# Hybrid attention step on one core: queries and keys transposed in fp32 and split from PSUM, context heads of a chunk in one operation

## The chip, the cores and the metric

The kernel runs on one core of a Trainium2 chip. TensorE (PE; its weight loads have a row of their own, PEld), VectorE (DVE), ScalarE (ACT) and GpSimd (POOL) work in parallel; SyncE (SP) issues the DMAs. The metric is the device time of one execution in microseconds (us), the median of several runs; below 0.5% a difference can't be told from none.

## The reference

One inference step with four layers over 128 context tokens and 512 latent tokens, width 1024, 16 query heads and 4 key/value heads of 64. Per layer:

```python
u = rms_norm(h, norm_pre) * (1 + scl) + shift          # scl, shift, gate from SiLU(cond) @ w_mod
q, k, v, z = split(u @ w_in)                            # 1024, 256, 256, 1024 columns
q, k = rms_norm per head (times q_norm / k_norm), rotary positions on latent tokens (layers 0, 1, 3)
o = softmax(q k^T / 8) v        # context tokens read context keys only;
                                # latent tokens read latent keys (all, a band, or a neighbourhood) and 128 cached context keys
h = h + gate * rms_norm((o * silu(z)) @ w_out, norm_post)
```

The keys and values of the context tokens are outputs too. All of it is fp32.

## The kernel before

**Precision.** TensorE takes a 32-bit type that it multiplies in one pass with rounded operands (F32R in the code, "fp32r"). The kernel splits each fp32 operand into a rounded part `hi` and a rest `lo` and adds the products of the parts, so each projection runs three fp32r matmuls for one. Weights are split as they arrive (`start_w`, helper `split`, lines 261 and 262), activations in `start_part` and `split_og`.

**Staging.** A layer runs `kv_chunk` (projection of keys and values for five token tiles of 128), then two chunks `c` of eight query heads and two key heads each: `q_chunk` (five token tiles), `z_block` (gate), four `lat_pair` (two heads each: scores, softmax, transposes of the probabilities, attention times values), and `ctx_heads` (the context tokens' own attention, two groups `gg` of four heads). After both chunks come `split_og` and `out_phase` (output projection, residual, and the next layer's input).

**Queries.** For each token tile `q_chunk` takes the normed queries `qn` [128 tokens, 8 heads, 64] in two halves of four heads. Per half ACT writes `hi` into `hl[:, :, 0:64]` (line 613), DVE or POOL writes `lo` into `hl[:, :, 64:128]` (line 615), PE transposes the four 128x128 blocks in fp32r into a PSUM tile (line 620), and one ACT or DVE copy of 512 columns brings it to `q` (line 256, helper `evac`). So `q[:, head]` has the 64 `hi` rows on partitions 0 to 63 and the 64 `lo` rows on 64 to 127.

**Keys.** `k_stack` makes one key tile for two key heads: `hi` and `lo`, each written twice side by side (lines 544 and 545, 256 columns each), four fp32r transposes (line 553), one copy of 512 columns to `kst[:, g, i, columns]` (`i` is 0 for `hi`, 1 for `lo`; both halves of the partitions hold the same 64 rows). A score is then two fp32r matmuls that accumulate, one with `hi` keys and one with `lo` keys. In chunk 0 `k_stack` is called from `kv_chunk`; the other two key heads are kept in `kn2` (line 591), and in chunk 1 six calls build a new `kst` from it (line 1001). There is one `kst` buffer.

**Context heads.** Per group `gg`: scores, softmax, four fp32 transposes (line 826), a copy, four fp32 matmuls of attention times values into a PSUM tile (line 834; two instructions each), and one DVE operation of 256 columns that multiplies the result into the gate (line 839).

**Order of the work.** Each operation is recorded by `S.op` with planned durations and the engines that may run it. `Sched.emit` then writes the program by a greedy list scheduling: each operation's due time is its running index plus an offset of its part (`ORDER`, as 'ks' -170, 'qt' -410), and it goes out when engines, buffers and dependencies allow by the planned times (`LAT`, `TURN`, `DISLIKE`). In `TURN` the kinds of PE work are M (fp32r matmul), R (fp32r transpose), T (fp32 transpose), C (attention times values), E (modulation). PSUM has four buffers "B", shared by projections, transposes and attention times values, and two "S". The order of every engine is therefore the planner's, and it is made anew when an operation is added or removed. All DMAs go through SP's queue in order of their issue.

## Time and profile before

Three runs: 1394.93, 1398.39 and 1403.29 us, median 1398.39. The profiled execution took 1400.58 us, of which 1398.5 us is the span from the first to the last instruction; 2.1 us lie around it.

| | busy us | share | instructions |
|---|---|---|---|
| PE matmul | 1357.7 | 97% | 9464 |
| PE weight load | 1122.3 | 80% | 9464 |
| DVE | 954.7 | 68% | 2300 |
| ACT | 758.6 | 54% | 1854 |
| POOL | 266.8 | 19% | 306 |

A matmul's record is longer than its turn on the engine, since consecutive ones overlap: the time that one costs is read from one start to the next in a timeline, not from its mean duration. The mean granted TensorE clock is 0.998 of 2.4 GHz.

### The profile page before, as it was taken

How to read it: one execution, taken by the hardware profiler on the slowest of the kernel's cores; microseconds unless marked ns; L12 is line 12 of the kernel's file. 1: busy time of each engine (PE TensorE's matmuls, PEld its weight loads, DVE VectorE, ACT ScalarE, POOL GpSimd, SP SyncE). 2: the span in 40 equal slices, each digit the busy share in tenths (PEclk: the TensorE clock that was granted, in tenths of full speed). 3: DMA queues.
4: the chain of work that ended last, by engine and by line, in shares of the span. 5: the costliest groups of instructions: out<-in, count | busy, mean ns of one | idle time of the engine just before them, and what ended most of it. 6: DMA issues, size and time to landing. Idle time of an engine off the chain costs nothing.

```text
span 1398.5 us, 25496 instructions
## 1 busy us (share of the span) xinstructions
PE 1357.7 (97%) x9464; PEld 1122.3 (80%) x9464; DVE 954.7 (68%) x2300; ACT 758.6 (54%) x1854; POOL 266.8 (19%) x306
## 2 busy tenths in 40 slices
PE   6999999999999999999999999999999999999998
PEld 3788887888778887887878888888778888778876
DVE  4777667765587786777486676578488876577653
ACT  4556565554355565666354567468345555465641
POOL 1122012010032102201033541441033210021100
PEclk9999999999999999999999999999999999999999
DMA  8522222224532402324542522342633210111032
GB/s 305 175 69 84 61 91 84 69 87 140 181 115 67 147 30 91 125 92 161 161 125 73 157 57 91 98 141 85 196 126 101 91 53 10 61 52 41 31 123 103
DMA packets 73323, 145.11 MB, mean 104 GB/s; under 512 B 8752, under 2 KB 13936, under 8 KB 73200
## 3 DMA queue, kind: packets, MB, share of 16 engines
q1 hardware_dynamic: 73200, 143.50, 31.6%
q8 instruction: 74, 1.21, 0.4%
q14 instruction: 49, 0.40, 0.1%
HBM read 131.90 MB, written 11.57 MB: 103 GB/s over the span
## 4 chain that ended last, share of the span: by engine, by line
PE 83%; DVE 6%; ACT 4%; DMA 3%; issue 3%; POOL 0%; SPq 0%; DVEq 0%; POOLq 0%; ACTq 0%
PE B L497 21%; PE B L634 14%; PE B L780 8%; PE B L773 8%; PE S L901 8%; PE B L901 6%; PE S L698 5%; PE S L724 4%; PE B L383 3%; PE B L620 2%; PE S L497 1%; DVE w L262 1%; DMA raw<-in_w_mod 1%; DMA raw<-in_w_in 1%; PE B L451 1%
## 5 line engine op out<-in xcount | busy, mean ns | idle before, releaser
L307 POOL TENSOR_TENSOR sm<-sm,mhalf 128x1 f32<-128x1 f32 (+2 forms) x100 | 122.1, 1223 | 573.2 <-DVE sm L302 291.5
L497 PE MATMUL B<-w,uB 128*128 128x512 f32 x816 | 207.4, 401 | 0.0
L256 ACT ACTIVATE pt<-B 128x512 f32<-128x512 f32 (+1 forms) x228 | 126.9, 570 | 121.0 <-PE B L773 110.8
L497 PEld LDWEIGHTS B<-w,uB 128*128 128x128 f32 x816 | 149.2, 188 | 31.8 <-DVE uB L262 0.4
L634 PE MATMUL B<-uB,w 128*128 128x384 f32 x768 | 166.0, 348 | 0.6 <-DVE gate L642 0.3
L773 PE MATMUL B<-ident,p 128*128 128x128 f32 x1088 | 159.4, 276 | 3.1 <-ACT pt L256 2.3
L261 ACT ACTIVATE w<-raw 128x512 fp32r<-128x512 f32 x224 | 135.0, 627 | 30.2 <-PE B L901 8.0
L773 PEld LDWEIGHTS B<-ident,p 128*128 128x128 f32 x1088 | 125.1, 141 | 23.7 <-issue 13.6
L262 DVE TENSOR_TENSOR w<-raw,w 128x512 fp32r<-128x512 f32 x193 | 130.5, 700 | 13.0 <-ACT w L261 12.4
L497 PE MATMUL B<-w,uA 128*128 128x512 f32 x528 | 135.1, 403 | 1.1 <-DVE pt L256 0.8
L703 ACT ACTIVATE p<-S,sm 128x640 f32<-128x640 f32 x128 | 101.3, 794 | 59.6 <-DVE sm L701 54.6
L780 PE MATMUL B<-pt,vt 128*64 128x256 f32 (+1 forms) x1152 | 133.0, 376 | 0.0
L634 PEld LDWEIGHTS B<-uB,w 128*128 128x128 f32 x768 | 129.6, 188 | 3.7 <-issue 1.5
L701 DVE TENSOR_REDUCE sm<-S 128x1 f32<-128x640 f32 x128 | 102.7, 819 | 37.7 <-PE S L698 36.8
L634 PE MATMUL B<-uA,w 128*128 128x256 f32 x768 | 117.6, 290 | 0.3 <-DVE modc L394 0.3
L497 PEld LDWEIGHTS B<-w,uA 128*128 128x128 f32 x528 | 96.4, 188 | 24.7 <-DVE w L262 2.1
L780 PEld LDWEIGHTS B<-pt,vt 128*64 128x64 f32 x1152 | 77.5, 137 | 46.0 <-issue 11.4
L634 PEld LDWEIGHTS B<-uA,w 128*128 128x128 f32 x768 | 102.5, 189 | 3.4 <-issue 1.8
L658 DVE TENSOR_SCALAR p<-p,sm 128x640 f32<-128x640 f32 (+2 forms) x197 | 96.9, 506 | 6.6 <-DVE sm L657 0.5
L698 PE MATMUL S<-kst,q 128*128 128x320 f32 x512 | 96.8, 320 | 2.9 <-ACT p L703 2.8
L658 POOL TENSOR_SCALAR p<-p,sm 128x640 f32<-128x640 f32 (+2 forms) x59 | 44.0, 751 | 284.3 <-DVE sm L657 236.4
L737 ACT ACTIVATE p<-p,sm 128x512 f32<-128x512 f32 (+1 forms) x128 | 83.9, 657 | 6.4 <-DVE sm L735 6.3
(148 smaller groups left out, 2216.1 us busy)
## 6 DMA issues: line engine op xcount, KB each, us to landing
raw<-in_w_in SPq DMA_DIRECT2D x160, 256.0 KB
raw<-in_w_mod SPq DMA_DIRECT2D x160, 256.0 KB
raw<-in_w_out SPq DMA_DIRECT2D x64, 256.0 KB
w<-in_w_first SPq DMA_DIRECT2D x16, 512.0 KB
xs<-q SPq DMA_DIRECT2D x15, 512.0 KB
q<-xs SPq DMA_DIRECT2D x15, 512.0 KB
q<-in_x SPq DMA_DIRECT2D x10, 512.0 KB
kst<-gs SPq DMA_DIRECT2D x8, 512.0 KB
```

The costliest lines, as they stand in the source:

```text
L256: alts = {"A": Ap(n, lambda e: e.activation(out(), in_(), AF.Copy)), "V": V(n, lambda e: e.tensor_copy(out(), in_()))}
L261: S.op([As(n, lambda e: e.activation(h(), src(), AF.Copy))], r, w)
L262: f = lambda e: e.tensor_sub(l(), src(), h().bitcast(F32))
L307: S.op([("G", 395 + 157 * n, lambda e: e.tensor_tensor(r.ap, v.ap, mhalf.ap.to_broadcast([128, n]), op=OP.pow), "pow")], r=[v, mhalf], w=[r])
L497: e.matmul(ps(), t.ap[:, s, k, off:off + 128], W[k].ap[:, w], start=k == 0 and i == 0, stop=k == 7 and i == 2)
L634: e.matmul(ps.ap[:, 0:w], W[k].ap[:, wi, 128 * f:128 * f + 128], t.ap[:, s, k, :], start=k == 0 and i == 0, stop=k == 7 and i == 2)
L658: f = lambda e, i=i, p=p, w=w: e.tensor_scalar(p.ap[:, 0:w], p.ap[:, 0:w], rs.ap[:, i:i + 1], 1.0, op0=OP.mult, op1=OP.mult)
L698: e.matmul(ps.ap[:, b, 0:320], Q[t + 1].ap[:, hh], kst.ap[:, g, s, 320 * b:320 * b + 320], start=s == 0, stop=s == 1)
L701: S.op([V(640, lambda e, ps=ps, i=i: e.tensor_reduce(negm.ap[:, i:i + 1], ps.ap[:, :, 0:320], axis=AX.XY, op=OP.max, negate=True))], r=[ps ...
L773: e.transpose(pt.ap[:, c:c + 128], p.ap[:, b:b + 128], ident.ap)
L780: e.matmul(po.ap[64 * x:64 * x + 64, 256 * half + q0:256 * half + q0 + w], vt.ap[:, kt, 64 * g:64 * g + 64], sbt.ap[:, c0:c0 + w], start=f ...
L901: e.matmul(ps(), t.ap[:, s, k, off:off + 128], W[k].ap[:, w], start=k == 0 and i == 0, stop=k == 7 and i == 2)
```

## The change

In `q_chunk` the fp32 queries themselves are transposed: four 128x128 blocks of two heads each, in fp32, into one PSUM tile. The parts are then made out of PSUM: for the even heads (x = 0, rows 0 to 63) ACT writes `hi` to `q` on the same rows and DVE writes `lo` to rows 64 to 127; for the odd heads (x = 1) `hi` is on rows 64 to 127 and `lo` on 0 to 63. Each of these four operations has 64 partitions and 512 columns. The scores wait for `(Q, hh % 2)` where they waited for `(Q, hh // 4)`.

In `k_stack` the source holds each key head twice side by side in fp32; two fp32 transposes fill half a PSUM tile, ACT writes `hi` (256 columns) and DVE `lo` (256 columns) to `kst`. The doubled source is made by an ACT copy of 256 columns into `kn2` (128 before), and for chunk 0 by a copy of 256 columns on ACT or DVE into a tile `kd`; cached keys are loaded twice, by four DMAs per layer in place of two. POOL has no part in the splits of queries and keys any more.

In `ctx_heads` the transposed probabilities of both groups are kept, the eight matmuls run as one operation into one PSUM tile, and one DVE operation of 512 columns multiplies the gate. `ORDER`, `TURN` and the other constants are as they were.

```diff
--- before.py
+++ after.py
@@ -538,32 +538,28 @@
     @S.named("ks")
     def k_stack(src, srckey, kst, ct, cap=None):
 
-        hl = tmp([128, 2, 2, 2, 64], F32R)
         tc_ = [cap, kst] if cap else [kst]
-        s = lambda: src()[:, :, None, :].to_broadcast([128, 2, 2, 64])
-        S.op([As(256, lambda e: e.activation(hl.ap[:, 0], s(), AF.Copy))], r=[srckey], w=[(hl, 0)], touch=tc_)
-        f = lambda e: e.tensor_sub(hl.ap[:, 1], s(), hl.ap[:, 0].bitcast(F32))
-        S.op([G(256, f), VL(256, f)], r=[srckey, (hl, 0)], w=[(hl, 1)], touch=tc_)
-        ps = S.buf("B", [128, 512], F32R)
+        ps = S.buf("B", [128, 512])
 
         def tr(e):
-            for i in range(2):
-                for g in range(2):
-                    c = 128 * (2 * i + g)
-                    e.transpose(ps.ap[:, c:c + 128], hl.ap[:, i, g].rearrange("p a d -> p (a d)"), identr.ap)
-        S.op([P(336, tr, "R")], r=[hl, identr], w=[ps], touch=tc_)
-        evac(512, lambda: kst.ap[:, :, :, 128 * COL[ct]:128 * COL[ct] + 128],
-             lambda: ps.ap.bitcast(F32).rearrange("p (i g c) -> p g i c", i=2, g=2), [ps], [(kst, ct)])
+            for g in range(2):
+                e.transpose(ps.ap[:, 128 * g:128 * g + 128], src()[:, g].rearrange("p a d -> p (a d)"), ident.ap)
+        S.op([P(218, tr, "T")], r=[srckey, ident], w=[ps], touch=tc_)
+        v = lambda: ps.ap[:, 0:256].rearrange("p (g c) -> p g c", g=2)
+        d = lambda i: kst.ap[:, :, i, 128 * COL[ct]:128 * COL[ct] + 128]
+        S.op([As(256, lambda e: e.activation(d(0), v(), AF.Copy))], r=[ps], w=[(kst, ct)])
+        S.op([V(256, lambda e: e.tensor_sub(d(1), v(), d(0).bitcast(F32)))], r=[ps, (kst, ct)], w=[(kst, ct)])
 
     def new_kst():
         return S.buf("kst", [128, 2, 2, 768], F32R)
 
     @S.named("kv")
     def kv_chunk(l, tabs, W):
-        kst, vt, kn2 = new_kst(), S.buf("vt", [128, 6, 256]), S.buf("kn2", [128, 6, 2, 64])
-        ck = tmp([128, 2, 64])
-        S.op([D(64, lambda e: e.dma_start(ck.ap, a["cache_k"][0, l, :, 0:2]))], w=[ck], touch=[kst])
-        S.op([D(64, lambda e: e.dma_start(kn2.ap[:, 4], a["cache_k"][0, l, :, 2:4]))], w=[(kn2, 4)])
+        kst, vt, kn2 = new_kst(), S.buf("vt", [128, 6, 256]), S.buf("kn2", [128, 6, 2, 2, 64])
+        ck = tmp([128, 2, 2, 64])
+        for x in range(2):
+            S.op([D(64, lambda e, x=x: e.dma_start(ck.ap[:, :, x], a["cache_k"][0, l, :, 0:2]))], w=[(ck, x)], touch=[kst])
+            S.op([D(64, lambda e, x=x: e.dma_start(kn2.ap[:, 4, :, x], a["cache_k"][0, l, :, 2:4]))], w=[(kn2, 4)])
         S.op([D(128, lambda e: e.dma_start(vt.ap[:, KC, :], a["cache_v"][0, l].rearrange("t h d -> t (h d)")))], w=[(vt, KC)])
         k_stack(lambda: ck.ap, ck, kst, 4)
         for tau in range(5):
@@ -588,9 +584,13 @@
             if tau == 0:
                 S.op([D(128, lambda e, kn=kn: e.dma_start(o["nk"][0, l], kn.ap))], r=[kn])
                 S.op([D(128, lambda e: e.dma_start(o["nv"][0, l].rearrange("t h d -> t (h d)"), vt.ap[:, VC, :]))], r=[(vt, VC)])
-            S.op([As(128, lambda e, kn=kn, ct=ct: e.activation(kn2.ap[:, ct], kn.ap[:, 2:4], AF.Copy))], r=[kn], w=[(kn2, ct)],
+            two = lambda k0, kn=kn: kn.ap[:, k0:k0 + 2, None, :].to_broadcast([128, 2, 2, 64])
+            S.op([As(256, lambda e, two=two, ct=ct: e.activation(kn2.ap[:, ct], two(2), AF.Copy))], r=[kn], w=[(kn2, ct)],
                  touch=[cap])
-            k_stack(lambda kn=kn: kn.ap[:, 0:2], kn, kst, ct, cap)
+            kd = tmp([128, 2, 2, 64])
+            S.op([As(256, lambda e, two=two, kd=kd: e.activation(kd.ap, two(0), AF.Copy)),
+                  V2(256, lambda e, two=two, kd=kd: e.tensor_copy(kd.ap, two(0)))], r=[kn], w=[kd], touch=[cap, kst])
+            k_stack(lambda kd=kd: kd.ap, kd, kst, ct, cap)
         return kst, vt, kn2
 
     @S.named("qt")
@@ -607,20 +607,20 @@
                 qn = rope(xr, 8, tabs, "q", tau - 1, cap)
             else:
                 qn = gscale(xr, 8, tabs, 0, cap)
-            for i in range(2):
-                hl, pt = tmp([128, 4, 128], F32R), S.buf("B", [128, 512], F32R)
-                s = lambda i=i, qn=qn: qn.ap[:, 4 * i:4 * i + 4]
-                S.op([As(256, lambda e, s=s, hl=hl: e.activation(hl.ap[:, :, 0:64], s(), AF.Copy))], r=[qn], w=[(hl, 0)],
-                     touch=[cap])
-                f = lambda e, s=s, hl=hl: e.tensor_sub(hl.ap[:, :, 64:128], s(), hl.ap[:, :, 0:64].bitcast(F32))
-                S.op([G(256, f), VL(256, f)], r=[qn, (hl, 0)], w=[(hl, 1)], touch=[cap])
-
-                def tr(e, hl=hl, pt=pt):
-                    for h in range(4):
-                        e.transpose(pt.ap[:, 128 * h:128 * h + 128], hl.ap[:, h], identr.ap)
-                S.op([P(336, tr, "R")], r=[hl, identr], w=[pt], touch=[cap])
-                evac(512, lambda i=i, q=q: q.ap[:, 4 * i:4 * i + 4].rearrange("p h t -> p (h t)"),
-                     lambda pt=pt: pt.ap.bitcast(F32), [pt], [(q, i)])
+            pt = S.buf("B", [128, 512])
+
+            def tr(e, pt=pt, qn=qn):
+                for pr in range(4):
+                    e.transpose(pt.ap[:, 128 * pr:128 * pr + 128], qn.ap[:, 2 * pr:2 * pr + 2].rearrange("p h d -> p (h d)"),
+                                ident.ap)
+            S.op([P(436, tr, "T")], r=[qn, ident], w=[pt], touch=[cap])
+            for x in range(2):
+                hi, lo = (slice(0, 64), slice(64, 128))[::1 - 2 * x]
+                d = lambda rows, x=x, q=q: q.ap.rearrange("p (r x) t -> p x r t", x=2)[rows, x]
+                v = lambda hi=hi, pt=pt: pt.ap[hi].rearrange("p (r t) -> p r t", r=4)
+                S.op([As(512, lambda e, d=d, v=v, hi=hi: e.activation(d(hi), v(), AF.Copy))], r=[pt], w=[(q, x)], touch=[cap])
+                S.op([V(512, lambda e, d=d, v=v, hi=hi, lo=lo: e.tensor_sub(d(lo), v(), d(hi).bitcast(F32)))], r=[pt, (q, x)],
+                     w=[(q, x)], touch=[cap])
             Q.append(q)
         return Q
 
@@ -697,7 +697,7 @@
                         for b in range(2):
                             e.matmul(ps.ap[:, b, 0:320], Q[t + 1].ap[:, hh], kst.ap[:, g, s, 320 * b:320 * b + 320],
                                      start=s == 0, stop=s == 1)
-                S.op([P(588, mm)], r=[(Q[t + 1], hh // 4)] + [(kst, x) for x in range(5)], w=[ps], seq="s")
+                S.op([P(588, mm)], r=[(Q[t + 1], hh % 2)] + [(kst, x) for x in range(5)], w=[ps], seq="s")
                 S.op([V(640, lambda e, ps=ps, i=i: e.tensor_reduce(negm.ap[:, i:i + 1], ps.ap[:, :, 0:320], axis=AX.XY, op=OP.max,
                                                                   negate=True))], r=[ps], w=[(negm, i)])
                 S.op([("A", 775, lambda e, ps=ps, p=p, i=i: e.activation(
@@ -722,7 +722,7 @@
                     for o, n, v in parts:
                         for s in range(2):
                             e.matmul(ps.ap[:, i, o:o + n], Q[t + 1].ap[:, hh], v(s), start=s == 0, stop=s == 1)
-                S.op([P(w * 0.88 + 14, mm)], r=[(Q[t + 1], hh // 4)] + [(kst, x) for x in BAND[t]], w=[(ps, i)], seq="s")
+                S.op([P(w * 0.88 + 14, mm)], r=[(Q[t + 1], hh % 2)] + [(kst, x) for x in BAND[t]], w=[(ps, i)], seq="s")
                 bb, bap = bias[t]
                 S.op([V(w, lambda e, i=i, w=w, p=p, bap=bap: e.tensor_tensor_reduce(
                     out=p.ap[:, 0:w], in0=ps.ap[:, i, 0:w], in1=bap(), op0=OP.add, op1=OP.max, scale=1.0, scalar=-3.0e38,
@@ -789,6 +789,7 @@
 
     @S.named("cx")
     def ctx_heads(l, c, Q, kst, vt, gate):
+        tiles = []
         for gg in range(2):
             g = 2 * c + gg
             ps = S.buf("S", [128, 2, 512])
@@ -798,7 +799,7 @@
                 for h in range(4):
                     for s in range(2):
                         e.matmul(psv()[:, h], Q[0].ap[:, 4 * gg + h], kst.ap[:, gg, s, 640:768], start=s == 0, stop=s == 1)
-            S.op([P(880, mm)], r=[(Q[0], gg), (kst, 5)], w=[ps], seq="s")
+            S.op([P(880, mm)], r=[Q[0], (kst, 5)], w=[ps], seq="s")
             negm, ssum, p = sm(4), sm(4), S.buf("p", [128, 4, 128])
             S.op([V(512, lambda e, psv=psv, negm=negm: e.tensor_reduce(negm.ap, psv(), axis=AX.X, op=OP.max, negate=True))],
                  r=[ps], w=[negm])
@@ -826,19 +827,22 @@
                     e.transpose(pt.ap[:, 128 * h:128 * h + 128], p.ap[:, h], ident.ap)
             S.op([P(432, tr, "T")], r=[p, ident], w=[pt])
             evac(512, lambda sbt=sbt: sbt.ap, lambda pt=pt: pt.ap, [pt], [sbt])
-            po, ocap = S.buf("B", [128, 512]), S.buf("cap_o")
-
-            def mv(e, po=po, sbt=sbt, g=g):
+            tiles.append(sbt)
+        po, ocap = S.buf("B", [128, 512]), S.buf("cap_o")
+
+        def mv(e):
+            for gg, sbt in enumerate(tiles):
+                g = 2 * c + gg
                 for h in range(4):
-                    x, b = h % 2, h // 2
+                    x, b = h % 2, 2 * gg + h // 2
                     e.matmul(po.ap[64 * x:64 * x + 64, 128 * b:128 * b + 128], vt.ap[:, VC, 64 * g:64 * g + 64],
                              sbt.ap[:, 128 * h:128 * h + 128], start=True, stop=True, skip_group_check=True)
-            S.op([P(505, mv, "C")], r=[sbt, (vt, VC)], w=[po], touch=[ocap])
-            gt = lambda g=g: gate.ap[:, 2 * g:2 * g + 2, 0:128]
-            keys = [(gate, (2 * g, 0)), (gate, (2 * g + 1, 0))]
-            S.op([V(256, lambda e, po=po, gt=gt: e.scalar_tensor_tensor(
-                gt(), po.ap[:, 0:256].rearrange("p (b q) -> p b q", b=2), 0.5, gt(), op0=OP.mult, op1=OP.mult))],
-                r=[po] + keys, w=keys, touch=[ocap])
+        S.op([P(1010, mv, "C")], r=tiles + [(vt, VC)], w=[po], touch=[ocap])
+        gt = lambda: gate.ap[:, 4 * c:4 * c + 4, 0:128]
+        keys = [(gate, (4 * c + b, 0)) for b in range(4)]
+        S.op([V(512, lambda e: e.scalar_tensor_tensor(
+            gt(), po.ap.rearrange("p (b q) -> p b q", b=4), 0.5, gt(), op0=OP.mult, op1=OP.mult))],
+            r=[po] + keys, w=keys, touch=[ocap])
 
     @S.named("tab")
     def tables(l):
```

## Rows read from the trace of the kernel before

**Rows 1.** The profile page: engine totals, and the 40 slices of the span (tenths) for PE and for the granted clock.

```profile
PE 1357.7 (97%) x9464; PEld 1122.3 (80%) x9464; DVE 954.7 (68%) x2300; ACT 758.6 (54%) x1854; POOL 266.8 (19%) x306
...
PE   6999999999999999999999999999999999999998
...
PEclk9999999999999999999999999999999999999999
```

**Rows 2.** The chain of work that ended last, by engine.

```profile
PE 83%; DVE 6%; ACT 4%; DMA 3%; issue 3%; POOL 0%; SPq 0%; DVEq 0%; POOLq 0%; ACTq 0%
```

**Rows 3.** Busy time in stretches: length, PE, PEld, DVE, ACT, POOL (instructions), granted clock, DMA share, GB/s. The first and last stretch of the span, two stretches of chunk 0's query projections, and the change from chunk 0 to chunk 1 in the last layer.

```profile
0.00:40.00 40.00, 28.41 (x178) 17.09 (x178) 21.08 (x67) 16.32 (x43) 4.93 (x12) 1.00 0.86 310
...
1335.00:1398.00 63.00, 56.81 (x252) 44.75 (x250) 26.50 (x47) 15.62 (x38) 2.77 (x5) 0.98 0.32 113
...
430.00:456.00 26.00, 26.00 (x131) 21.30 (x130) 16.94 (x34) 11.10 (x23) 6.65 (x4) 1.00 0.10 30
...
1084.00:1103.00 19.00, 19.00 (x97) 15.77 (x96) 14.49 (x29) 9.42 (x20) 4.95 (x3) 1.00 0.12 36
1185.00:1205.00 20.00, 17.33 (x123) 14.31 (x121) 9.40 (x20) 14.46 (x41) 0.00 (x0) 0.91 0.09 28
```

**Rows 4.** The chain from 1335 us to the end, in order of time: start, us, what. L901 is the output projection (fp32r, 512 columns), L834 a group of context heads.

```profile
1338.95 0.59 PE B L834 x8
1339.54 0.89 PE S L901 x3
1340.43 0.59 PE B L834 x8
1341.02 22.68 PE S L901 x96
1363.70 22.51 PE B L901 x96
```

**Rows 5.** Timeline of PE in layer 0's first query projections (L497, fp32r, 512 columns): start, us, what. L620 are the fp32r transposes of queries.

```profile
85.46 0.46 PE L620 MATMUL B<-identr,tmp 128*128 128x128 f32 x4
85.76 0.94 PE L497 MATMUL B<-w,uB 128*128 128x512 f32 x3
86.53 0.45 PE L620 MATMUL B<-identr,tmp 128*128 128x128 f32 x4
86.83 4.43 PE L497 MATMUL B<-w,uB 128*128 128x512 f32 x18
91.10 0.46 PE L620 MATMUL B<-identr,tmp 128*128 128x128 f32 x4
```

**Rows 6.** Timeline of PE in the second layer boundary. L451 are fp32 transposes (of the next layer's input), four at a time.

```profile
706.40 2.34 PE L901 MATMUL B<-w,uB 128*128 128x512 f32 x9
708.58 0.60 PE L451 MATMUL B<-ident,p 128*128 128x128 f32 x4
708.93 0.95 PE L901 MATMUL B<-w,uB 128*128 128x512 f32 x3
709.72 1.57 PE L497 MATMUL B<-w,uA 128*128 128x512 f32 x6
```

**Rows 7.** Timeline of PE at the start, where fp32 transposes (L451) come two at a time.

```profile
45.17 0.38 PE L451 MATMUL B<-ident,q 128*128 128x128 f32 x2
45.30 0.95 PE L497 MATMUL B<-w,uB 128*128 128x512 f32 x3
46.09 0.38 PE L451 MATMUL B<-ident,q 128*128 128x128 f32 x2
```

**Rows 8.** Groups of instructions by line and form over the whole span: out<-in, shape, count, busy us, mean ns, then the idle time of the engine before them.

```profile
L613 ACT ACTIVATE tmp<-tmp 128x256 fp32r<-128x256 f32 x80 | 29.5, 410 | 68.1 <-DVE tmp L534 41.9 <-DVE tmp L528 26.0
...
L615 DVE TENSOR_TENSOR tmp<-tmp 128x256 fp32r<-128x256 f32 x78 | 32.2, 435 | 12.9 <-ACT tmp L613 12.7
...
L256 ACT ACTIVATE q<-B 128x512 fp32r<-128x512 f32 x78 | 45.0, 595 | 31.9 <-PE B L620 31.6
...
L544 ACT ACTIVATE tmp<-tmp 128x256 fp32r<-128x256 f32 x24 | 10.0, 415 | 15.9 <-DVE tmp L528 5.8 <-DVE tmp L534 4.4 <-DMA tmp<-in_cache_k 4.2
L544 ACT ACTIVATE tmp<-kn 128x256 fp32r<-128x256 f32 x24 | 7.8, 425 | 0.0
L545 DVE TENSOR_TENSOR tmp<-kn,tmp 128x256 fp32r<-128x256 f32 x22 | 9.7, 504 | 0.0
L545 DVE TENSOR_TENSOR tmp<-tmp 128x256 fp32r<-128x256 f32 x23 | 9.6, 420 | 4.2 <-ACT tmp L544 4.0
L256 ACT ACTIVATE kst<-B 128x512 fp32r<-128x512 f32 x44 | 25.4, 597 | 14.1 <-PE B L553 13.4
L256 DVE CAST kst<-B 128x512 fp32r<-128x512 f32 x4 | 2.7, 686 | 0.9 <-PE B L553 0.9
L591 ACT ACTIVATE kn<-tmp 128x128 f32<-128x128 f32 x20 | 6.0, 298 | 0.0
...
L945 DVE TENSOR_TENSOR tmp<-B,kst 128x512 f32<-128x512 f32 x20 | 13.7, 687 | 21.0 <-ACT tmp L943 21.0
L839 DVE SCALAR_TENSOR_TENSOR gate<-B,gate 128x256 f32<-128x256 f32 x16 | 6.7, 420 | 13.4 <-PE B L834 13.4
L256 ACT ACTIVATE pm<-B 128x256 f32<-128x256 f32 x5 | 1.9, 381 | 7.6 <-PE B L346 7.5
L256 ACT ACTIVATE pm<-B 128x128 f32<-128x128 f32 x11 | 3.0, 277 | 16.8 <-PE B L383 16.8
L412 ACT ACTIVATE gsb<-B 16x128 f32<-16x128 f32 x4 | 1.0, 251 | 0.0
```

**Rows 9.** The line of the cached keys' first DMA: its issue on SP, ns (min/median/max), and who waited for it.

```profile
L565 SPq DMA_DIRECT2D tmp<-in_cache_k x4: 328/424/426, 37.5 to 1049.6; - x4
...
  ACT tmp L544: 4.2, 3
```

## The prediction

> **What bounds the kernel now.** I read the page first: the engine totals and the slices [rows 1]. The reader is to see that PE is busy for 97% of the span and in nine tenths or more of every slice but the first and the last, at a clock that is full in all of them, while DVE and ACT have 68% and 54%. Then the chain of waits [rows 2]: 83% of the way to the end is PE work, and what DVE and ACT add (10%) is scattered. Then the stretches [rows 3]: of PE's 1398.5 - 1357.7 = 40.8 us of idle time, 11.6 lie in the first 40 us and 6.2 in the last 63, which leaves 23 us for everything between. So a PE turn that goes away in the middle shortens the span by about its length, if the planner finds other work to put there; and a longer DVE or ACT operation costs nothing until it makes PE wait. Last I read what a turn costs, from one start to the next in the timelines, because the mean duration of a matmul holds its way through the array as well.
>
> **The change part by part.** The yardstick is the fp32r matmul of 512 columns: 96 in 22.51 us, 0.2345 us each [rows 4].
>
> An fp32r block of four transposes: from its start to the next matmul 0.30 us, twice, and the three matmuls behind the first take 0.77 us where three are worth 0.70, the 18 behind the second 4.27 for 4.22 [rows 5]. With that loss of about 0.06 a block costs 0.36 us.
>
> An fp32 block of four: 0.35 us to the next start, and the three matmuls behind it take 0.79 for 0.70 [rows 6]. I take 0.35 + 0.09 = 0.44. A block of two: 0.13 us, and again 0.79 for the next three [rows 7], so 0.22.
>
> Queries: 4 layers x 2 chunks x 5 tiles = 40 times, two fp32r blocks (0.72) become one fp32 block of four (0.44): 40 x 0.28 = 11.2 us off PE. Keys: per layer one tile from the cache, five from the projection and six in chunk 1, 48 in all; a block of 0.36 becomes one of 0.22: 48 x 0.14 = 6.7 us. If the trailing losses were not PE's own but chance, the blocks would be 0.60 against 0.35 and 0.30 against 0.13, which is 10.0 + 8.2, about the same.
>
> Context heads: two blocks of 0.59 us, with 0.89 for the three matmuls between them (0.19 too much) and 22.68 for 22.51 behind the second (0.17) [rows 4]. In one operation the 0.59 stays twice and one of the two losses goes: 0.19 x 8 chunks = 1.5 us. The bounds are nothing, if a chunk's two groups would have run next to each other or now wait for the second group's softmax, and 8 x 0.36 = 2.9 us.
>
> PE in sum: 11.2 + 6.7 + 1.5 = 19.4 us.
>
> DVE and ACT [rows 8]. Queries: DVE loses its subtractions (32.2 us) and two copies, some 1.4, and gets 80 subtractions of 512 columns from PSUM. No row has one on 64 partitions. The nearest of the same form is L945, 687 ns; by half the rows it could be half of that, but an ACT copy of 128 columns took 251 ns on 16 partitions and 277 on 128, so the columns set it, and I take 687: 80 x 0.687 = 55.0, which is 21.4 us more. (At half: 27.5, 6 us less than before.) ACT loses 29.5 + 45.0 and gets 80 x 0.595 = 47.6: 26.9 less. Keys: DVE loses 9.7 + 9.6 + 2.7 and gets 48 of 0.420 (as L839, one operand in PSUM) = 20.2, so 1.8 less; ACT loses 10.0 + 7.8 + 25.4 and gets 48 of 0.381 = 18.3, 24.9 less; the wider copy into kn2 adds 20 x 0.415 - 6.0 = 2.3 on ACT, and the 20 copies into kd at most 20 x 0.42 = 8.4 on either. The gates: 8 x 0.687 - 6.7 = 1.2 less on DVE. Together DVE gains 18 to 27 us, to about 975 us or 71%, and ACT loses 41 to 50, to about 713. PE's remaining work covers both. In a stretch of query projections DVE is the tighter one: 14.49 of 19 us [rows 3], with room for some 0.5 us more per tile; what that costs if the cover is gone is the third rival.
>
> What is late next: the PSUM tile of the queries. Now two tiles per token tile are each held for the transposes and one copy, 0.46 [rows 5] + 0.595 us, 2.1 in sum. Afterwards one is held for 0.60 [rows 6] + 0.595 + 0.595 + 0.687 = 2.5 us, because the two ACT copies run one after the other and the last subtraction follows. Tile-time rises by a fifth, without a new peak. Behind the waiting subtraction on DVE stand the next tile's norm and rotation, and PE waits for these only through the next tile's transposes. An odd or even head's scores now need half of that one tile, all four transposes, so a chunk's first scores come later than with the first of two blocks; the gate projections are there to fill PE.
>
> The DMAs: four for two, per layer. Their issue is 0.33 to 0.43 us on SP [rows 9], 8 more are about 3 us of a queue that waits for buffers most of the time. ACT waited 4.2 us in all for the cached keys; that can be nothing, or rise by the second issue, 0.4 us x 4 = 1.6 us, most of it where PE has other work. I take zero.
>
> Against the profiled execution: 1400.6 (span 1398.5 and 2.1 around it) - 19.4 = 1381.2. The profiled run stands 2.2 us above the median, so the median becomes **1379 us**.
>
> One rule speaks against it. Fp32 transposes stand at 0.13 us for two and 0.35 for four [rows 6, 7], 0.065 and 0.09 us each. The Trainium skill, "FP8 and Floating Point Precision" (TensorE Precision Notes), says that true fp32 takes four passes through the array; by that an fp32 transpose of 128 columns costs as much as 512 columns in one pass, and the sum turns round (the fourth rival). The trace does not agree for transposes, and the skill's "TensorE: Matmul & The Clock Gate" (Terms) has the reason: a transpose mode that is four times faster for fp32.
>
> **The rivals.**
> 1. *More than the sum.* Between the chunks of the last layer PE is idle for 2.7 of 20 us and the clock falls to 0.91 on average [rows 3]: there the six key tiles are split, transposed and copied, ACT doing 6 x 0.42 + 6 x 0.60 = 6.1 us. Afterwards ACT has 6 x 0.38 = 2.3 and DVE 2.5, and the transposes need no split before them. If that wait goes (2.7 + 0.09 x 20 = 4.5 us) and half as much in the three other layers in sum, the time is 1372. Against it: the same ACT is not full there, 14.46 of 20.
> 2. *The new order is worse.* The offsets of the parts count operations, and a query tile now records fewer of them, so everything behind shifts against its due time. For it: nothing in the profile protects the 23 us of idle time in the middle from growing. If it grows by half, 11.5 us, the time is 1391.
> 3. *DVE becomes the bound of the query stretches, slower than before.* The subtractions out of PSUM come last on the way to the scores and hold the tile. If PE waits for one of them per token tile, that is 40 x 0.687 = 27.5 us, and 1407. It decides from 19.4 / 40 = 0.49 us of waiting per tile. For it: 76% DVE in 19 us, which becomes 85% with two tiles more at 0.54 us. Against it: the other stretch has 65% [rows 3], and four PSUM tiles let PE go ahead.
> 4. *Fp32 transposes of queries and keys are dearer than those in the trace*, as dear as 512 columns of an fp32r matmul, 0.2345 us each [rows 4]: a query block 4 x 0.2345 + 0.09 = 1.03 (0.31 more than now, x 40 = 12.4), a key block 0.56 (0.20 more, x 48 = 9.6), less 1.5: 1419. Against it: every fp32 transpose in the trace [rows 6, 7].
>
> **How the numbers follow.** Forecast 0.58, its own range 1372 to 1388; more than the sum 0.07; the worse order 0.20; DVE 0.12; dearer transposes 0.03. 0.5% (7 us) is what a measurement of this kernel can tell from none, so faster means under 1391.4: the forecast, the first rival and half of the second, 0.75. Slower, over 1405.4: dearer transposes and over half of DVE, 0.10. Between them 0.15. The range reaches from 1367, below the first rival, to 1397, above the second, and leaves out most of the third and the fourth.
>
> **What would show it.** Right: PE's matmul busy time falls by 19 us or more with the idle time in the middle at 23 us or so; fp32 transposes of queries at 0.35 us to the next start; ACT near 713, DVE near 975 us; subtractions on 64 partitions at 0.69 us. Wrong: PE waiting for the subtractions out of PSUM in the query stretches; a fallen clock in more than one place; or transposes of 0.23 us each.

## The result, and the profile after

The changed kernel takes 1413.52 us (median of 4 runs, 1412.67 to 1414.15) against 1398.37: ratio 1.0101 (95% interval 1.0081 to 1.0120). By the ratio it is slower by 14 us where the prediction had 19 us less. The profiled execution took 1412.67 us, its span 1410.9.

The page of the kernel after: engine totals, the shares of the chain by engine, and the granted clock by slice.

```profile
PE 1353.6 (96%) x9208; PEld 1107.4 (78%) x9208; DVE 983.5 (70%) x2304; ACT 720.6 (51%) x1753; POOL 252.8 (18%) x287
...
PEclk9999999999999999999999998999999999999999
...
PE 77%; DVE 10%; ACT 4%; DMA 4%; issue 3%; POOL 1%; SPq 0%; DVEq 0%; POOLq 0%; ACTq 0%
```

Against [rows 1] PE has 256 matmuls fewer, but its busy time fell by 4.1 us only and its idle time rose from 40.8 to 1410.9 - 1353.6 = 57.3. DVE's part of the chain went from 6% to 10% [rows 2], and PE's fell to 77%.

Groups of the kernel after by line and form, in the columns of [rows 8]: the subtractions and copies of queries (L622, L621), and those of keys (L551, L550).

```profile
L622 DVE TENSOR_TENSOR q<-B,q 64x512 fp32r<-64x512 f32 x80 | 55.1, 689 | 25.6 <-ACT q L621 24.0
L621 ACT ACTIVATE q<-B 64x512 fp32r<-64x512 f32 x80 | 47.3, 592 | 43.2 <-PE B L614 42.5
...
L551 DVE TENSOR_TENSOR kst<-B,kst 128x256 fp32r<-128x256 f32 x48 | 19.4, 419 | 10.0 <-ACT kst L550 9.7
L550 ACT ACTIVATE kst<-B 128x256 fp32r<-128x256 f32 x48 | 17.8, 382 | 14.8 <-PE B L546 14.6
```

The durations of the single operations came as forecast. What PE waited for in the kernel after (us in all, times, longest):

```profile
PE B L346 <- DMA w<-in_w_first: 9.3, 2, 7.2
PE B L546 <- DVE kst L551: 5.1, 8, 1.6
PE B L614 <- DVE tmp L528: 4.4, 8, 0.8
PE B L634 <- DVE q L622: 3.8, 3, 1.3
...
PE S L698 <- DVE q L622: 0.8, 2, 0.4
...
PE B L773 <- DVE kst L551: 0.8, 2, 0.5
PE S L724 <- DVE q L622: 0.7, 2, 0.5
```

Three of the first four are DVE: the key transposes wait for a PSUM tile that the subtraction L551 still holds, the query transposes for the rotation before them (L528, on DVE too), and the gate projection (L634) for a tile that L622 holds. The waits for the two new subtractions, L551 and L622, make 11.2 us in all. In the kernel before, the waits of PE for the copies in their place (L256 to `kst` and `q`) made 1.0 us:

```profile
PE B L773 <- ACT kst L256: 0.4, 1, 0.4
...
PE B L553 <- ACT kst L256: 0.4, 1, 0.4
...
PE B L634 <- ACT kst L256: 0.2, 1, 0.2
```

One such wait, on the timeline of the kernel after (in order of start; start, us, what, and in brackets the idle time before it):

```profile
1254.93 0.63 PE L614 MATMUL B<-ident,tmp 128*128 128x128 f32 x4 [0.22 <-ACT pt L256]
...
1255.60 1.20 ACT L621 ACTIVATE q<-B 64x512 fp32r<-64x512 f32 x2
...
1255.97 0.68 DVE L262 TENSOR_TENSOR w<-raw,w 128x512 fp32r<-128x512 f32 x1
...
1256.83 1.39 DVE L622 TENSOR_TENSOR q<-B,q 64x512 fp32r<-64x512 f32 x2 [0.18 <-ACT q L621]
...
1258.25 0.82 DVE L701 TENSOR_REDUCE sm<-S 128x1 f32<-128x640 f32 x1
...
1258.37 1.54 PE L634 MATMUL B<-uB,w 128*128 128x384 f32 x4 [1.28 <-DVE q L622]
```

The transposes of this tile began at 1254.93 and DVE ended with it at 1258.22: held for 3.3 us, not 2.5. The two copies (L621) and the two subtractions (L622) ran one after the other: DVE was done with its weight split (L262) at 1256.65 and stood idle for 0.18 us until the second copy had ended. The 2.5 of the prediction had the first subtraction beside the second copy. Over the 40 tiles, the first subtraction began only behind the second copy in 36, mostly with DVE idle before it (the 24.0 us of idle time in the row of L622), and the hold is 3.3 us in the median. In 35 tiles the record of the first copy updates no semaphore (the signal that another engine waits for), so that nothing tells DVE of its end: the tile is held by the length of this chain, and not by a queue in front of DVE.

The change from chunk 0 to chunk 1 of layer 2 on PE (L546 are key transposes), and a window of it beside the window of the kernel before that has its own change of chunk, with key transposes (L553) from 854 to 861 us (columns as in [rows 3]; the first is after, the second before):

```profile
867.85 0.38 PE L546 MATMUL B<-ident,kn 128*128 128x128 f32 x2
869.81 0.44 PE L546 MATMUL B<-ident,kn 128*128 128x128 f32 x2 [1.58 <-DVE kst L551]
871.18 0.44 PE L546 MATMUL B<-ident,kn 128*128 128x128 f32 x2 [0.93 <-DVE kst L551]
```

```profile
870.00:880.00 10.00, 6.95 (x30) 4.42 (x31) 4.40 (x8) 4.02 (x8) 1.56 (x1) 0.64 0.00 0
```

```profile
855.00:865.00 10.00, 9.49 (x68) 7.18 (x66) 4.24 (x10) 7.62 (x21) 1.96 (x2) 1.00 0.00 0
```

PE waits for one key tile after the other, and behind these waits its granted clock falls: 0.64 on average, part of the window at 1.2 GHz. In full stretches of 20 us the profile after has six with a clock under 1.00, which cost 10.4 us in sum; before there was one (1.8 us). So of the 31.8 us between the forecast (19.4 less) and the profile (12.4 more), 16.5 are PE's idle time and up to 8.6 the clock (some of it falls on idle time); the rest is at least 6.7. The turns of the three changed groups did fall by 17.0 us, summed over the timelines from start to next start without idle time (queries 27.1 to 16.0, keys 17.1 to 12.4, context heads 9.4 to 8.2). Those of other groups rose: the gate projections (L634) by 6.9, the projections (L497) by 2.9, scores (L724) by 2.1, in part at the lower clock. Why the rest of them rose stays open.

### The profile page after: what moved, and what is told of

The parts are those of the page before. It is cut to its first block, busy times and chain, and to the rows that moved or that the text cites. A ratio compares the mean times of both kernels' runs of the same rounds, so it can differ in the third digit from the quotient of the medians.

```text
span 1410.9 us, 24794 instructions
## 1 busy us (share of the span) xinstructions
PE 1353.6 (96%) x9208; PEld 1107.4 (78%) x9208; DVE 983.5 (70%) x2304; ACT 720.6 (51%) x1753; POOL 252.8 (18%) x287
## 3 DMA queue, kind: packets, MB, share of 16 engines
q1 hardware_dynamic: 76400, 144.02, 31.8%
## 4 chain that ended last, share of the span: by engine, by line
PE 77%; DVE 10%; ACT 4%; DMA 4%; issue 3%; POOL 1%; SPq 0%; DVEq 0%; POOLq 0%; ACTq 0%
PE B L497 16%; PE B L634 13%; PE B L780 9%; PE B L773 8%; PE S L905 7%; PE B L905 6%; PE S L698 5%; PE S L724 4%; PE B L383 3%; DMA raw<-in_w_mod 2%; PE S L497 2%; DVE q L622 1%; DVE tmp L463 1%; DVE w L262 1%; ACT w L261 1%
## 5 line engine op out<-in xcount | busy, mean ns | idle before, releaser
L497 PE MATMUL B<-w,uB 128*128 128x512 f32 x816 | 204.7, 400 | 0.1
L256 ACT ACTIVATE pt<-B 128x512 f32<-128x512 f32 (+1 forms) x222 | 123.0, 568 | 114.8 <-PE B L773 98.3
L497 PEld LDWEIGHTS B<-w,uB 128*128 128x128 f32 x816 | 150.1, 188 | 32.7 <-DVE uB L262 0.5
L634 PE MATMUL B<-uB,w 128*128 128x384 f32 x768 | 169.0, 353 | 4.3 <-DVE q L622 3.8
L262 DVE TENSOR_TENSOR w<-raw,w 128x512 fp32r<-128x512 f32 x196 | 133.3, 702 | 12.2 <-ACT w L261 11.5
L634 PEld LDWEIGHTS B<-uB,w 128*128 128x128 f32 x768 | 132.7, 193 | 7.1 <-issue 5.5
L497 PE MATMUL B<-w,uA 128*128 128x512 f32 x528 | 135.2, 404 | 1.6 <-ACT pt L256 1.1
L634 PE MATMUL B<-uA,w 128*128 128x256 f32 x768 | 119.8, 290 | 1.3 <-DVE w L262 1.2
L497 PEld LDWEIGHTS B<-w,uA 128*128 128x128 f32 x528 | 96.9, 189 | 25.9 <-DVE w L262 1.8
L634 PEld LDWEIGHTS B<-uA,w 128*128 128x128 f32 x768 | 102.7, 189 | 4.9 <-DVE w L262 2.6
L658 DVE TENSOR_SCALAR p<-p,sm 128x640 f32<-128x640 f32 (+2 forms) x207 | 102.0, 508 | 6.3
L658 POOL TENSOR_SCALAR p<-p,sm 128x640 f32<-128x640 f32 (+2 forms) x49 | 37.1, 767 | 302.8 <-DVE sm L657 264.7
```

What stands on the lines that cost most here:

```text
L256: alts = {"A": Ap(n, lambda e: e.activation(out(), in_(), AF.Copy)), "V": V(n, lambda e: e.tensor_copy(out(), in_()))}
L262: f = lambda e: e.tensor_sub(l(), src(), h().bitcast(F32))
L497: e.matmul(ps(), t.ap[:, s, k, off:off + 128], W[k].ap[:, w], start=k == 0 and i == 0, stop=k == 7 and i == 2)
L634: e.matmul(ps.ap[:, 0:w], W[k].ap[:, wi, 128 * f:128 * f + 128], t.ap[:, s, k, :], start=k == 0 and i == 0, stop=k == 7 and i == 2)
L658: f = lambda e, i=i, p=p, w=w: e.tensor_scalar(p.ap[:, 0:w], p.ap[:, 0:w], rs.ap[:, i:i + 1], 1.0, op0=OP.mult, op1=OP.mult)
```

## The experiments

Theory A: PE's turns did fall, and DVE gives the time back, because the subtraction out of PSUM now stands between transposes and scores and holds the tile. Rivals: the planner's new order and its due times; the price of single operations on half the partitions; the clock by itself. Each ratio is to runs of the kernel before on the same chip.

**One part at a time.** Of the diff, e1_q has only the queries, e2_k only the keys, e3_cx only the context heads, e13_kcx keys and context heads.

> Only the queries are transposed in fp32 and split from PSUM; keys and context heads as before. Theory 1 (the subtraction out of PSUM on DVE now stands between the transposes and both the release of the PSUM tile and the scores, so that PE waits for DVE's queue): the queries carry most of the loss, about 2/3 of the +15 us: 1405 to 1412, with PE waits on the new subtraction line. Theory 2 (any new set of operations makes the greedy planner write another order, worse by chance): time anywhere, not proportional to the part; PE waits spread over other lines. By the prediction's sum alone (11 us off PE): 1387.

> Only the keys are transposed in fp32 and split from PSUM. Theory 1: about 1/3 of the loss, 1398 to 1406, with PE waits on the key subtraction at the start of chunk 1, where six key tiles go through four PSUM buffers. Theory 2: anywhere between 1385 and 1410. By the sum alone (6.7 us off PE): 1392.

> Only the context heads of a chunk in one operation. Both theories: little, 1395 to 1402; by the sum alone 1397. If it alone costs 5 us or more, the loss is where both groups' softmax is waited for at the end of a chunk, and theory 1 is wrong on the place.

> The keys and the context heads changed, the queries as before. From the single parts (0.9994 and 0.9985 of the kernel before) 0.998 of it, 1396 to 1400; by the sum of the prediction 8 us less. If the parts only cost together, over 1403.

| | median us | ratio | 95% interval |
|---|---|---|---|
| e1_q | 1408.66 | 1.0047 | 1.0029 to 1.0065 |
| e2_k | 1400.70 | 0.9994 | 0.9981 to 1.0007 |
| e3_cx | 1399.13 | 0.9985 | 0.9969 to 1.0001 |
| e13_kcx | 1398.54 | 0.9998 | 0.9978 to 1.0017 |

The queries alone cost 6.6 us where 11.2 less were forecast; keys and context heads give nothing that can be told, alone or together. The three add up to 0.26%, the whole costs 1.01%: the parts make each other worse. They share DVE, PSUM and the planner's order; which of these does it, the parts don't show. In e1_q PE waits 5.1 us for L528 and 3.9 for L622, as in the whole (its profile is of its fastest run, 1401.39 us). In e2_k PE waits little for the keys' subtraction. It waits more for the cached keys, whose transposes now come straight behind the DMAs; in the kernel before this wait was ACT's [rows 9]:

```profile
PE B L546 <- DMA tmp<-in_cache_k: 3.5, 4, 1.5
...
PE B L546 <- DVE kst L551: 1.2, 4, 0.4
```

**The tile's hold.** e4_copy first copies the tile out of PSUM (512 columns, ACT or DVE) and splits from the copy; e7_copypool lets POOL take the subtractions too.

```diff
+qs = tmp([128, 4, 128])
+evac(512, ... qs ..., ... pt.ap, [pt], [qs])
-v = lambda hi=hi, pt=pt: pt.ap[hi].rearrange("p (r t) -> p r t", r=4)
+v = lambda hi=hi, qs=qs: qs.ap[hi]
```

> The changed kernel, but the transposed queries are first copied from PSUM to SBUF by one operation of 512 columns (ACT or DVE, some 24 us more work in all), and both parts are made from that copy: the PSUM tile no longer waits for the two ACT copies and the subtractions. Theory 1, if it is the held tile: faster than the changed kernel by 5 to 12 us (1402 to 1408) in spite of more work; if it is the later scores: slower, 1415 to 1422, since the way to the scores is one operation longer. Theory 2: anywhere.

> As the run with the copy out of PSUM (1409.6), and POOL may make the queries' lower parts as well, as in the kernel before. Theory 1 with DVE's load as the cause: 1400 to 1407, POOL taking some of the 80 subtractions. If DVE's load is not what counts: 1408 to 1414.

1409.64 us, 1.0047 (1.0028 to 1.0066), and 1408.28, 1.0073 (1.0052 to 1.0094). Releasing the tile early gives back about half of the loss at best, for 40 copies more, and the 5.1 us of PE waits for L551 stay. In e7_copypool POOL took only 4 of the 80 subtractions, so it tells little of DVE's load.

**The order.** e5_due counts the due times as if the missing operations were still recorded (3 a query tile, 1 a key tile of chunk 1, 2 for the context heads); e6_cost tells the planner the measured 592, 689, 382 and 419 ns; e9_prio makes the splits due 300 earlier.

> The changed kernel with the due times put back: the planner's running index advances as if the operations that the change removed were still there (3 per query tile, 1 per key tile of chunk 1, 2 per chunk's context heads), so every part is due where it was in the kernel before. Theory 2 in its narrow form (the offsets of the parts no longer fit): back to 1395 to 1403. Theory 1 (PE waits for the subtractions out of PSUM): 1408 to 1418, with the same waits.

> The changed kernel with the planner told what the four new operations take on the chip (592 and 689 ns for a query's half, 382 and 419 ns for a key's, where it assumed 520, 598, 306 and 332). Theory 3 (the planner thinks these operations done earlier than they are and lets PE stand on them): 1400 to 1408, with the waits of PE on the subtractions cut by half. Theory 1 without the planner's part in it: 1410 to 1418.

> The changed kernel with the split of queries and keys due 300 operations earlier, so that ACT and DVE take it before other work that waits. Theory 1, if it is the place in DVE's queue: 1402 to 1409. If it is the length of the chain of four operations itself: no change, 1411 to 1417.

1.0066 (1.0044 to 1.0087), 1.0065 (1.0045 to 1.0086) and 1.0100 (1.0082 to 1.0119). Two of the other orders are worth some 5 of 14 us (e10_guard's, below, 7), the third nothing, and none of the four brings the gain: the order is a part of the loss, and whether some other order would take away the rest isn't shown. By its expectation e9_prio speaks against DVE's queue: with the splits due earlier nothing changes, which fits the length of the chain of four operations and not their place in the queue.

**The quadrant change.** Each new subtraction of queries reads one half of the 128 partitions and writes the other (a quadrant is a quarter of them). On the timeline after, two L622 take 1.42 us from the first's start to the next operation (1256.83 to 1258.25), while operations of 689 ns in a row start 0.60 us apart. To see what this costs, e10_guard records both ACT copies before both subtractions, and three kernels keep e10_guard's order instruction for instruction: e11_full does all four operations on 128 partitions in place, e12_short has the copies on 128 partitions and subtractions of half the columns, e15_wide has the copies on 128 and the subtractions as they were. The queries of e11_full hold lower parts only, and e12_short leaves out half of the lower parts, so the scores of these two are not the reference's.

```diff
-S.op([As(512, ... e.activation(d(hi), v(hi), AF.Copy))], ...)
+S.op([As(512, ... e.activation(d(al), v(al), AF.Copy))], ...)    # al = slice(0, 128)
-... e.tensor_sub(d(lo), v(hi), d(hi).bitcast(F32))
+... e.tensor_sub(d(al), v(al), d(al).bitcast(F32))
```

> The changed kernel, only that both ACT copies of a query tile go before its two subtractions. It is the base of the next two runs, which have the same program in the same order on every engine. 1408 to 1416.

> As the base before it, instruction for instruction, but the four operations of a query tile take all 128 partitions and stay on them, in place of 64 partitions that change from the lower half to the upper one; the queries so made hold lower parts only, so the scores are not the reference's. Theory 4 (a half-height operation that changes partitions costs DVE and ACT some 0.1 us more of their time, because it does not overlap its neighbours: two subtractions take 1.42 us from start to the next start in the changed kernel, where two full ones take 1.2): 4 to 10 us faster than the base. Theory 1 without it (the order and the place of the subtraction): within 2 us of the base.

> As the base, instruction for instruction, with the copies on all 128 partitions and each subtraction of a query tile cut to half its columns (256 of 512; the odd pairs of heads keep rounded rows in place of lower parts, so the scores are not exact). It takes 80 x 0.27 = 21 us of DVE time away and nothing else. Theory 1 (PE waits for DVE's late subtractions): 8 us or more faster than the base. If DVE's time is not what PE waits for: within 3 us.

> e10_guard with both ACT copies on all 128 partitions, so that no copy changes quadrants; the subtractions stay on 64 partitions and 512 columns. Same order, instruction for instruction. Theory (the quadrant change costs where DVE makes it, since PE waits for the subtractions; ACT has room): within 3 us of e10_guard, 1404 to 1410. Rival (ACT's changes cost as much as DVE's): 1400 or less, half of the way to e11_full. If e15_wide stands at e12_short (1399.5), it was the copies, and the shortening told nothing.

| | median us | ratio | 95% interval |
|---|---|---|---|
| e10_guard | 1406.89 | 1.0050 | 1.0030 to 1.0070 |
| e11_full | 1397.78 | 0.9998 | 0.9977 to 1.0019 |
| e12_short | 1399.49 | 0.9988 | 0.9969 to 1.0006 |
| e15_wide | 1405.00 | 1.0037 | 1.0020 to 1.0054 |

The same four DVE operations in e10_guard and in e11_full:

```profile
103.73 0.68 DVE L624 TENSOR_TENSOR q<-B,q 64x512 fp32r<-64x512 f32 x1
104.43 0.82 DVE L704 TENSOR_REDUCE sm<-S 128x1 f32<-128x640 f32 x1
105.28 0.69 DVE L624 TENSOR_TENSOR q<-B,q 64x512 fp32r<-64x512 f32 x1
106.00 0.69 DVE L510 TENSOR_TENSOR tmp<-B,sm 128x512 f32<-128x512 f32 x1
```

```profile
106.34 0.68 DVE L624 TENSOR_TENSOR q<-B,q 128x512 fp32r<-128x512 f32 x1
106.94 0.81 DVE L704 TENSOR_REDUCE sm<-S 128x1 f32<-128x640 f32 x1
107.68 0.67 DVE L624 TENSOR_TENSOR q<-B,q 128x512 fp32r<-128x512 f32 x1
108.27 0.67 DVE L510 TENSOR_TENSOR tmp<-B,sm 128x512 f32<-128x512 f32 x1
```

Durations are the same to 0.02 us; the starts are not: 2.27 us to L510 against 1.93. The subtraction and the operation behind it each start only when the one before has ended, some 0.11 us later each time, and no row of durations shows it. Over all the places where these operations follow each other without a wait it makes 10.9 us of DVE (its busy time is 981.9 us in e10_guard and 971.2 in e11_full), and taking it away gives 0.52% (7 us). The copies' own changes give 0.13% (e15_wide), with intervals that overlap: it is DVE's subtractions that carry the price. In e12_short they still change halves, but DVE is busy for 20 us less than in e15_wide (962.2 against 982.2), and that gives 0.49% (7 us): DVE's time in these operations does reach PE. Against the kernel after, e10_guard has another order: PE has no idle time before query transposes (5.1 us after), so the waits for L528 belong to the order; and it is faster although a query tile is held longer (3.6 us in the median), so the hold alone doesn't set the time.

**The keys, once more.** e14_kold is e11_full with the keys as before (its queries hold lower parts only, too). e16_pair is e15_wide with chunk 1's six key tiles built as three pairs, and e17_kcxpair is e13_kcx with the same pairs; queries are as before in it.

```diff
-for ct in (4, 5, 0, 1, 2, 3):
-    k_stack(lambda ct=ct, kn2=kn2: kn2.ap[:, ct], (kn2, ct), kst, ct)
+for cts in ((4, 2), (3, 5), (0, 1)):
+    k_pair(kn2, kst, cts)    # 4 transposes into 512 columns, one copy and one subtraction of 512
```

> e11_full with the keys made as before (split in SBUF, fp32r transposes, POOL among the engines of the subtraction); queries and context heads as in e11_full, so the low halves of the queries are left out here too. Theory (the new key build gives back all that its cheaper transposes save, by waits of PE for L551 and the clock behind them): the time stays within 4 us of e11_full, 1394 to 1401, PE's waits for L551 (5.1 us) are gone and its turns grow by some 6 us. Rival (the keys' 6.7 us did arrive, and it is the queries alone that fall short): 1403 to 1406. Second rival (the key build costs more than it saves): under 1393, which would beat the kernel before.

> e15_wide, and in chunk 1 the six key tiles are built as three pairs: four fp32 transposes fill a whole PSUM tile, one ACT copy and one subtraction of 512 columns take it to two neighbouring key tiles. Per layer 3 pairs of 0.595 and 0.687 in place of 6 of 0.382 and 0.419: 0.5 us less ACT and 0.45 us less DVE, half the PSUM tiles. Theory (PE waits in the rebuild because each tile is held for copy and subtraction one after the other): the waits for the keys' subtraction fall from 5.1 to under 3 us, and the time by 3 to 6 us against e15_wide. Rival (the wait is for the single kst buffer, or for the transposes' input, and pairs don't help): within 2 us of e15_wide, or more, since a pair comes later than a single tile.

> e13_kcx (keys and context heads changed, queries as before), with chunk 1's key tiles in pairs as in e16_pair. Theory (the keys' cheaper transposes are given back by waits and clock in the rebuild): 1393 to 1396, ahead of the kernel before, with PE's waits for the keys' subtraction under 1.5 us (2.4 in e13_kcx). Rival (the new order's loss lies elsewhere): 1397 to 1401, as e13_kcx.

| | median us | ratio | 95% interval |
|---|---|---|---|
| e14_kold | 1391.43 | 0.9942 | 0.9922 to 0.9962 |
| e16_pair | 1399.00 | 0.9998 | 0.9979 to 1.0016 |
| e17_kcxpair | 1392.78 | 0.9951 | 0.9935 to 0.9966 |

In e14_kold my theory was too mild and the second rival came: under e11_full's queries the new key build, with the order that follows from it, costs 0.56% (8 us) where it should save 6.7. Taken in turn, another order (e10_guard, 0.51%), no quadrant change (e11_full, 0.52%) and the old keys (e14_kold, 0.56%) lead from 14 us more than before to 8 us less; what is left of the change there, queries and context heads, was forecast at 12.7 less. Not all of the keys' 8 us lie at the keys: in the profiles (of runs of 1402.59 and 1390.43 us) PE is idle for 49.7 us in e11_full and 40.9 in e14_kold, of which 8.9 and 6.7 are before key transposes. The waits of PE by key operations in e11_full, then in e16_pair:

```profile
PE B L546 <- DVE kst L551: 5.1, 8, 1.5
```

```profile
PE B L561 <- DVE kst L567: 1.9, 3, 0.7
...
PE B L846 <- DVE kst L567: 1.4, 1, 1.4
```

(In e15_wide the row is 5.1, 8 times, too.) Pairs halve the copies, subtractions and PSUM tiles of the rebuild; the key transposes' own waits go from 5.1 to 1.9 us, one of 1.4 stands before the context heads' transposes (L846) instead, and 0.39% comes back against e15_wide. With queries as before, pairs make the keys' gain arrive. The page of e17_kcxpair, and its window over layer 2's change of chunk (key transposes from 853 to 856 us):

```profile
PE 1346.9 (97%) x9368; PEld 1114.1 (80%) x9368; DVE 948.6 (68%) x2279; ACT 743.8 (53%) x1822; POOL 255.6 (18%) x299
...
PE 83%; DVE 6%; DMA 4%; ACT 3%; issue 2%; POOL 1%; SPq 0%; DVEq 0%; POOLq 0%; ACTq 0%
```

```profile
850.00:860.00 10.00, 10.00 (x69) 8.11 (x68) 5.48 (x15) 6.91 (x25) 0.69 (x1) 1.00 0.21 78
```

PE is idle for 44.2 us (1391.1 of span less 1346.9), DVE has its old share, and no full stretch of 20 us has a clock under 1.00. This version leaves nothing out and is ahead of both kernels: 6.9 us less than before by the ratio, where keys and context heads were forecast at 8.2.

**The clock** was not changed by itself. Over the timed runs the time lost to it (each run's time by one less its mean granted clock, median) is 4.2 to 4.9 us before, 12.0 after, 5.6 in e13_kcx and 2.8 in e17_kcxpair, but also 11.2 in e11_full and 9.8 in e14_kold, which are no slower than the kernel before. So it doesn't set the time alone, and what it costs by itself isn't shown. How much of e13_kcx's step to e17_kcxpair (5.8 us by the medians) is wait and how much clock can't be told exactly; by these numbers 2.8 is the clock.

## Why the prediction was wrong

**What held.** *PE's turns.* From each query transpose to the next matmul's start, summed over the timelines without idle time, 27.1 us became 16.0 us, 0.40 a block for the 0.35 to 0.44 forecast; a key block stands at 0.14. The context heads' matmuls take 1.02 in one operation where two of 0.59 and a gap stood. The fourth rival is out. *Durations*: 689 ns for a subtraction on 64 partitions (687 taken), 592, 419, 382 as taken; ACT 720.6 (713), DVE 983.5 (975).

**What failed.** The step is "PE's remaining work covers both", with "a longer DVE or ACT operation costs nothing until it makes PE wait" behind it. I weighed DVE by its share of a stretch (76% of 19 us, 85% after; over the same 19 us it is 82%) and the tile by its hold (2.1 to 2.5 us), and found room in both. But a subtraction that is the last step before a PSUM tile comes free or scores can start makes PE wait whatever DVE's share: PE waited 11.2 us for L551 and L622 where 1.0 stood, and its idle time rose by 16.5 us though DVE's share is only 70%. The hold was mis-sized: it is 3.3 us, since both subtractions run behind both copies, so tile-time rises by more than half and not by a fifth.

**A term that was missing.** The subtractions were priced at their duration. Each also kept itself and the operation behind it from overlapping: some 0.11 us each time, 10.9 us of DVE in sum, and 7 us of the time (e11_full against e10_guard). The Trainium skill, "VectorE: DVE Perf Modes", section "Two Vector instructions with no wait between them", states the condition, as a model: an instruction whose input or output starts in another quadrant of partitions than the last one in that memory starts only when all earlier Vector instructions have finished. The diff shows that reading rows 0 to 63 and writing rows 64 to 127, and then the reverse, meets it each time. The trace agrees: 0.70, 0.85 and 0.72 us from start to start in e10_guard are 0.60, 0.74 and 0.59 in e11_full. The price is from these runs alone.

**The keys' term**: 6.7 us less was forecast; with the queries as before none of it arrived (e2_k), and under e11_full's queries it was 8 more (e14_kold). The first rival said that the wait between the chunks would go, as ACT had less to do. With the new queries it grew: ACT copy and DVE subtraction of a tile now run one after the other while it is held, where one copy released it. PE's waits for L551 (5.1 us) show this, its idle time before key transposes went from 3.8 to 9.3 us in all, and with pairs (e16_pair) it is 6.4. With the old queries the row of L551 is 1.2 us only, and PE's waits for the cached keys' DMAs, which I took as zero, are 3.5 (e2_k). The pairs of e17_kcxpair bring the gain; what else took it in e2_k and e13_kcx stays open.

**The rivals.** The third had the right place and side, but not its form. There is no wait in every query tile: PE waited for L622 seven times, 5.3 us in all. The loss is in fewer and longer waits, on L528 and L551 as well, and in the clock behind them. The second (order) holds in so far as other orders of the same operations were 5 to 7 us faster. "A fallen clock in more than one place" was named as what would show it wrong, but no price was put on it: up to 8.6 us in the profile. The chance of 0.10 for slower was too small, since three of the bounds (DVE, the hold, the clock) all point the same way once PE waits, and I counted them as separate.

## What to carry to other kernels

When work moves from before a transpose to behind it, the operations that do it then hold PSUM and stand ahead of the consumers: price the whole chain, from the transpose to the last of them, as it runs one after the other, and not by an engine's share of the stretch. Look in the diff for operations that read one part of the partitions and write another, and read their cost from start to start. Small PSUM tiles with a copy and then a subtraction each can be worth joining (three pairs for six tiles turned no gain into 0.5%).

## What the hardware showed that was not expected

Two neighbouring subtractions of 64x512 that change halves take 1.42 us to the next start, two full ones 1.20 (e11_full), though each is recorded at 0.68 to 0.69. ACT shows a smaller one: two copies of alternating halves take 1.20 us to the second's end and two of 128 partitions 1.09 (0.11 a pair), and no gain in time from this can be told (e15_wide). In the kernel after, the granted clock fell to 1.2 GHz in or behind single waits of PE of 1.3 us (ended at 241.6 and 1258.4) and behind groups of waits before key transposes (1.58, 0.93 and 0.81 us up to 872.4; 0.52, 0.35, 0.35 and 0.18 us up to 1207.2), and the stretches of 20 us there have 0.82 to 0.96, 1.8 us lost at a time where it is 0.91. Not every such wait was followed by a fall: 1.27 us at 412.2 in the kernel after and 1.28 at 299.0 in e17_kcxpair were not.
